# A half-product stage of a decoder layer: VectorE's low parts and token sums emitted in another place

## The chip, the core and the metric

The kernel runs on one core of one Trainium2 chip. The metric is the device time of one execution in microseconds (us). The engines are named as in the profile: PE is TensorE (PEld its weight loads), DVE is VectorE, ACT is ScalarE, POOL is GpSimd, SP is SyncE, which here only issues transfers.

## The reference

One layer of a hybrid decoder on 512 tokens of width 1024, in float32. A first sub-layer mixes tokens (RWKV-7 and sparse attention side by side); the change does not touch it. The second is a gated MLP with a short causal convolution:

```python
h = rms_norm(x, norm_ffn_pre[l])
u = causal_dwconv(h @ ffn_up[l], ffn_conv_w[l], ffn_conv_b[l])   # width 3, 2 * D_FF channels
u_gate, u_val = jnp.split(u, 2, axis=-1)
x = x + rms_norm((jax.nn.silu(u_gate) * u_val) @ ffn_down[l], norm_ffn_post[l])
```

D_FF is 2816, so the up projection makes 44 blocks of 128 channels, 22 for the gate and 22 for the value, and the kernel takes them as 22 pairs.

## The kernel before, in words

**Float32 out of two parts.** Every operand of a large product is kept as a high part and a low part: ACT copies the raw tile into a rounded type (the high part), and DVE or POOL subtracts that from the raw tile (the low part). A product is then three matmuls: high by high, high by low, low by high. So each weight tile costs one transfer, one ACT operation and one subtraction before PE can use it.

**The up projection.** Pairs 0 to 9 are computed directly. Pairs 10 to 21 (`SEVEN`) are computed by `seven` with seven half-size products in place of eight: tokens and weights are split in halves, sums and differences of weight halves (made earlier by transfers that add, `fsum`) are multiplied with sums and differences of token halves (`forms`), and the four quarters of the result are combined from the seven products. For pair j the weight forms are called `swj5, swj2, swj1, swj3, swj6, swj4, swj8`, in the order in which PE takes them. Each product is 12 matmuls of 128x128 by 128x256 (line 1567). The accumulators in PSUM are g (`sg` in the profile, the gate), v (`sv`, the value) and two helpers t[0], t[1] (`st`).

The seven products go: g left, t[0], v right, t[1], g left again, g right, t[1] again. Between them DVE combines (`add`, line 1572): u2 = t[0] - u2 (where ACT copied g left to u2 first), u4 = v + u2, v right = t[1] + u4, g right = g - u4, v left = t[1] + u2. In the profile u2 and u4 are `su`. The seventh product adds into t[1], so PE may start it only when DVE has read t[1] for v right; this is the one place in the loop where PE waits for DVE inside a pair.

**Weight forms.** `form_w` (line 1537 on) loads a form, and `split_to` makes its two parts: the high part on ACT (line 134), the low part on POOL for five of the seven (5, 2, 3, 6, 4) and on DVE for two (1 and 8), all on line 172. Eight buffers hold the forms, five in one pool and three in another, and a buffer comes free when PE has finished the product that used it. Five forms are begun before the first product; then each product begins one more (`next(coming)` in `prod`).

**After a pair.** The convolution: for g, then for v, ACT writes u (line 1619) and DVE adds two shifted products (lines 1620, 1621, `u<-sg,cvec,u` and `u<-sv,cvec,u`). Then ACT takes silu of the gate (line 1633), DVE multiplies gate and value into y (line 1635, `sv<-u,sg`), ACT makes its high part ah (line 1638), and DVE its low part al (line 1639). From pair 11 on three DVE operations make the token sums t24 for the down projection (lines 1647 to 1649, `t` in the profile), which SP stores to DRAM one pair later (line 1645).

**The order of the work.** The kernel is written as a program, and a scheduler puts each engine's instructions in a fixed order from dependences, the place where they are written, and estimated times; operations passed to `keep` stay in the order in which they are written. Each engine then runs its list strictly in order and waits by semaphores. Beside the loop POOL issues the transfers that sum the down weights (`ws`, line 272, `ds` in the profile); SP issues all weight loads. After pair 21 the down projection (`dn`, lines 1745 to 1747) begins at once.

Of the kernel before, what the change touches and what calls it, by code (L numbers as in the profile page):

```python
# [10 lines left out]
F32 = mybir.dt.float32  # L11
F32R = mybir.dt.float32r
AF = mybir.ActivationFunctionType
OP = mybir.AluOpType
# [4 lines left out]
S = 512  # L19
# [33 lines left out]
def hybrid_layer(ctx: ExitStack, tc: tile.TileContext, a, out, dbg=None, stop=None):  # L53
# [112 lines left out]
    def split_to(src, hi, lo, name, n, eng=None, p=None, late=False, tag="raw", bufs=RAWB):  # L166
        raw = (p or wp).tile([128, n], F32, tag=tag, name=name + "r", bufs=bufs)
        sy.dma_start(raw, src)
        i = act(hi, raw, AF.Copy)
        if late:  # L170
            tc.keep_in_program_order(i)
        (eng or po).tensor_tensor(lo, raw, hi.bitcast(F32), op=OP.subtract)
# [1306 lines left out]
    with pool("ff") as ff:  # L1479
# [58 lines left out]
        def form_w(src, name, eng):  # L1538
            n = next(ring)
            p_, tags, b = (wp, ("raw", "whi", "wlo"), (RAWB, WB)) if n % 8 % 3 == 1 else (sw, ("sraw", "shi", "slo"), (4, 5))  # L1540
            hi = p_.tile([128, 512], F32R, tag=tags[1], name=name + "h", bufs=b[1])
            lo = p_.tile([128, 512], F32R, tag=tags[2], name=name + "l", bufs=b[1])
            split_to(src, hi, lo, name, 512, eng, p_, late=n < 5, tag=tags[0], bufs=b[0])
            return hi, lo

        def form_seq():
            for j in SEVEN:
# [10 lines left out]
        def seven(j):  # L1558
            def tok(r, c):
                return quarter(h2h, r, c), quarter(h2l, r, c)  # L1560

            def prod(p, x, first=True, last=True):
                w = ahead.pop(0)
                for k in range(hf):
                    ks = slice(k * 128, k * 128 + 128)
                    for n, (y, z) in enumerate(((0, 0), (0, 1), (1, 0))):
                        te.matmul(p, w[y][:, ks], x[z][:, k, :], start=first and k + n == 0,  # L1567
                                  stop=last and k == hf - 1 and n == 2, skip_group_check=True)
                next(coming, None)

            def add(o_, x, y, op=OP.add):
                ve.tensor_tensor(o_, x, y, op=op)

            g, v, t = (pj if j % 2 else px)(f"sg{j}"), (pj if j % 2 else py)(f"sv{j}"), [pz(f"st{j}{i}") for i in range(2)]
            u2, u4 = (sw.tile([128, 256], F32, tag=f"u{i}", name=f"su{i}{j}", bufs=1) for i in (2, 4))
            prod(g[:, lft], tok(0, 0))
            prod(t[0][:, lft], forms[1])
            sc.activation(u2, g[:, lft], AF.Copy)
            add(u2, t[0][:, lft], u2, OP.subtract)
            prod(v[:, rgt], forms[0])  # L1580
            add(u4, v[:, rgt], u2)
            prod(t[1][:, rgt], forms[2])
            prod(g[:, lft], tok(1, 0), first=False)
            add(v[:, rgt], t[1][:, rgt], u4)
            prod(g[:, rgt], tok(1, 1))
            add(g[:, rgt], g[:, rgt], u4, OP.subtract)
            prod(t[1][:, rgt], forms[3], first=False)
            add(v[:, lft], t[1][:, rgt], u2)
            return g, v

        side = token_forms()
        sctx2 = ExitStack()
        for j in range(22):
            us = []
            sv_ = None
            if j == 2:
                sw = pool("sw", "right", sctx2)
            if j == SEVEN[0]:
                for _ in side:
                    pass  # L1600
            if j in SEVEN:
                sv_ = seven(j)
            for x in range(2):
                blk = 2 * j + x
                if blk < NU:
                    p = pu4[blk]
                    half_up(blk, 1)
                elif sv_ is not None:
                    p = sv_[x]
                else:  # L1610
                    wh, wl = after.get(blk) or split_w(upw(blk), f"up{blk}")
                    p = ((pj, px, py, pz)[blk % 4] if j < SEVEN[0] else pj)(f"pu{blk}")
                    mm3(p, wslice(wh), wslice(wl), lambda k: h2h[:, k, :], lambda k: h2l[:, k, :])
                if blk == 2 * SEVEN[0] - 1:
                    for _ in range(5):
                        next(coming)
                cv = blk * 4
                u = fu.tile([128, S], F32, tag=f"u{x}", name=f"u{blk}", bufs=2)
                sc.activation(u, p, AF.Identity, scale=cvec[:, cv + 2:cv + 3], bias=cvec[:, cv + 3:cv + 4])  # L1619
                ve.scalar_tensor_tensor(u[:, 1:], p[:, :S - 1], cvec[:, cv + 1:cv + 2], u[:, 1:], op0=OP.mult, op1=OP.add)  # L1620
                ve.scalar_tensor_tensor(u[:, 2:], p[:, :S - 2], cvec[:, cv:cv + 1], u[:, 2:], op0=OP.mult, op1=OP.add)
                us.append(u)
                if j < SEVEN[0]:
                    for _ in range(1):
                        next(side, None)
                if (j > 2 or x == 0 if j < SEVEN[0] else x == 0 and j < 19):
                    next(ws, None)
            if sv_ is None:
                sc.activation(us[0], us[0], AF.Silu)
                (ve if j > SEVEN[0] - 3 else po).tensor_tensor(us[1], us[0], us[1], op=OP.mult)  # L1630
                y = us[1]
            else:
                sc.activation(sv_[0], us[0], AF.Silu)
                y = sv_[1] if j >= KH else us[1]
                ve.tensor_tensor(y, us[1], sv_[0], op=OP.mult)
            if j < KH:
                ve.tensor_tensor(y[:, rgt], y[:, rgt], y[:, lft], op=OP.subtract)
            sc.activation(ah[:, j, :], y, AF.Copy)
            ve.tensor_tensor(al[:, j, :], y, ah[:, j, :].bitcast(F32), op=OP.subtract)
            if j >= KH:  # L1640
                if j == KH:
                    t2ctx = ExitStack()
                    t2 = pool("t2", "left", t2ctx)
                else:
                    sy.dma_start(t24d[j - 1 - KH], t24)
                t24 = t2.tile([128, S], F32, tag="t24", name=f"t24{j}", bufs=2)
                ve.tensor_tensor(t24[:, lft], y[:, rgt], ah[:, j - KH, rgt].bitcast(F32), op=OP.subtract)
                ve.tensor_tensor(t24[:, lft], t24[:, lft], al[:, j - KH, rgt].bitcast(F32), op=OP.subtract)
                ve.tensor_tensor(t24[:, rgt], y[:, lft], t24[:, lft], op=OP.subtract)
            if j == 1:  # L1650
                f4ctx.close()
        po.dma_start(t24d[21 - KH], t24)
        ring = itertools.count()

# [264 lines left out]
```

## Time and profile before

| | us |
|---|---|
| median of 3 runs | 1137.9 (1136.57 to 1139.19) |
| the profiled execution | 1133.54, its span 1131.5 |
| pairs 10 to 21, from 899.08 to 1019.15 of the span | 120.1 |
| PE busy over the span | 1110.3 (98%) |
| DVE, ACT, POOL busy over the span | 750.4, 639.2, 613.5 |

The profile is one execution with the time and length of each instruction, and a chain of work that ended last, followed back from the end. An engine's instruction begins in the record a little before its neighbour ends, since they overlap by some 0.08 us on DVE; so a length of time on an engine is best read from start to start. Durations on POOL are rough. The program's tiles carry numbers in the kernel that the profile mostly leaves out: `sv<-st,su` is the read of t[1] for v right and, later in the same pair, the one for v left.

### The profile page before, as it was taken

What the parts mean: (1) busy time and instruction counts of PE and PEld (TensorE: products, weight loads), DVE (VectorE), ACT (ScalarE), POOL (GpSimd) and SP (SyncE); (2) the same over time, 40 slices, a digit from 0 to 9 for tenths busy, and PEclk for the clock granted to TensorE, in tenths of its full rate; (3) what the DMA queues carried; (4) which work ended last, traced back from release to release, by engine and by line L of the source; (5) the groups of instructions that cost most, each with busy time, mean ns of one, the idle gap of its engine ahead of it and who ended that gap; (6) DMA issues with size and microseconds to landing.
All of it is one profiled execution on the core that took longest, in us unless ns stands there. A gap on an engine that the chain in (4) does not pass through costs nothing.

```text
span 1131.5 us, 21237 instructions
## 1 busy us (share of the span) xinstructions
PE 1110.3 (98%) x7704; PEld 909.6 (80%) x7704; DVE 750.4 (66%) x1432; ACT 639.2 (56%) x1258; POOL 613.5 (54%) x615
## 2 busy tenths in 40 slices
PE   9999999999999999999999999999999999999997
PEld 7888888877888887766666777888888899998885
DVE  4236664735666552597787754755785699997986
ACT  6447763554666434386675654543554576665554
POOL 4346674535666453566545543540578777753431
PEclk9999999999999999999999999999999999999999
DMA  7524468632666896516576465777568678968783
GB/s 256 144 81 124 141 166 217 182 104 86 182 146 172 235 242 216 132 48 194 171 218 181 127 149 166 231 240 220 136 185 202 207 263 227 266 181 302 228 283 113
DMA packets 117002, 208.33 MB, mean 184 GB/s; under 512 B 37025, under 2 KB 39905, under 8 KB 110754
## 3 DMA queue, kind: packets, MB, share of 16 engines
q1 hardware_dynamic: 93538, 144.05, 40.6%
q0 software_dynamic: 7504, 48.50, 18.4%
q10 hardware_dynamic: 15856, 14.42, 4.0%
q8 instruction: 61, 1.00, 0.4%
q14 instruction: 43, 0.35, 0.1%
HBM read 179.60 MB, written 72.35 MB: 223 GB/s over the span
## 4 chain that ended last, share of the span: by engine, by line
PE 87%; DVE 5%; DMA 3%; POOL 2%; issue 1%; ACT 1%; SPq 0%; DVEq 0%; POOLq 0%; ACTq 0%
PE st L1567 4%; PE sg L1567 3%; PE dn L1745 3%; PE dn L1746 3%; PE dn L1747 3%; PE gt L348 3%; PE o L1218 3%; PE gt L349 3%; PE gt L350 3%; PE pt L150 3%; PE ub L1276 3%; PE pu L234 2%; PE ub L1278 2%; PE pu L232 2%; PE pu L233 2%; PE ub L1277 2%
## 5 line engine op out<-in xcount | busy, mean ns | idle before, releaser
L1166 ACT ACTIVATE p<-p,stt 128x384 f32<-128x384 f32 (+3 forms) x128 | 70.6, 554 | 33.4 <-DVE stt L1164 30.8
L1164 DVE CUSTOM_DVE_ANT_0 p<-s,rh 128x384 f32<-128x384 f32 (+3 forms) x128 | 59.2, 484 | 21.5 <-PE s L1150 17.9
L1138 POOL TENSOR_SCALAR p<-p,stt 128x512 f32<-128x512 f32 (+1 forms) x64 | 39.3, 622 | 38.7 <-DVE stt L1131 24.5
L1746 PE MATMUL dn<-hl,ah 128*128 128x512 f32 x148 | 57.6, 389 | 0.0
L1747 PE MATMUL dn<-hh,al 128*128 128x512 f32 x148 | 57.6, 389 | 0.0
L1745 PE MATMUL dn<-hh,ah 128*128 128x512 f32 x148 | 57.2, 389 | 0.0
L150 PE MATMUL pt<-ident,p 128*128 128x128 f32 x320 | 44.3, 273 | 1.2 <-DVE p L1140 1.2
L1157 PE MATMUL s<-kst,qs 128*128 128x512 f32 (+1 forms) x128 | 38.8, 394 | 5.8 <-DVE stt L1164 5.6
L150 PEld LDWEIGHTS pt<-ident,p 128*128 128x128 f32 x320 | 37.8, 141 | 6.9 <-DVE p L1140 1.6
L1218 PE MATMUL o<-PT,vt 128*64 128x384 f32 (+3 forms) x256 | 41.0, 443 | 0.0
L1209 ACT ACTIVATE PT<-pt 128x512 f32<-128x512 f32 x48 | 27.5, 587 | 10.4 <-PE pt L150 10.3
L1157 PEld LDWEIGHTS s<-kst,qs 128*128 128x128 f32 x128 | 21.2, 189 | 15.0 <-DVE stt L1164 11.8
L1140 DVE TENSOR_SCALAR p<-p,stt 128x512 f32<-128x512 f32 (+1 forms) x64 | 32.3, 532 | 0.7
L1747 PEld LDWEIGHTS dn<-hh,al 128*128 128x128 f32 x148 | 27.8, 188 | 5.8
L1745 PEld LDWEIGHTS dn<-hh,ah 128*128 128x128 f32 x148 | 27.8, 188 | 5.8
L1746 PEld LDWEIGHTS dn<-hl,ah 128*128 128x128 f32 x148 | 27.8, 188 | 5.7
L1218 PEld LDWEIGHTS o<-PT,vt 128*64 128x64 f32 x256 | 16.3, 136 | 18.3 <-issue 16.0
L272 POOL DMA_DIRECT2D ds<-in_down_dram x36 | 25.6, 710 | 7.3 <-DMA ds<-ds 7.3
L1620 DVE SCALAR_TENSOR_TENSOR u<-pu,cvec,u 128x511 f32<-128x511 f32 x20 | 15.0, 748 | 19.2 <-ACT u L1619 19.2
L1211 DVE COPY PT<-pt 128x512 f32<-128x512 f32 x32 | 21.8, 680 | 8.6 <-PE pt L150 8.5
L251 POOL DMA_DIRECT2D fs<-in_up_dram x36 | 26.0, 731 | 0.5 <-issue 0.4
L868 ACT ACTIVATE UV<-xs 64x256 f32<-64x256 f32 x16 | 6.0, 378 | 35.7 <-PE xs L861 35.3
(2206 smaller groups left out, 4242.4 us busy)
## 6 DMA issues: line engine op xcount, KB each, us to landing
fs<-in_up_dram POOLq DMA_DIRECT2D x36, 512.0 KB, 6.5
ds<-in_down_dram POOLq DMA_DIRECT2D x30, 512.0 KB, 6.1
fs<-fs POOLq DMA_DIRECT2D x12, 512.0 KB, 4.4
ds<-ds POOLq DMA_DIRECT2D x10, 512.0 KB, 5.7
gtd<-gt ACTq DMA_DIRECT2D x16, 256.0 KB, 4.8
qs<-qd SPq DMA_DIRECT2D x32, 128.0 KB, 3.6
g<-gtd SPq DMA_DIRECT2D x16, 256.0 KB, 3.6
t24d<-t SPq DMA_DIRECT2D x10, 256.0 KB, 5.4
```

The costliest lines, as they stand in the source:

```text
L150: return te.transpose(o, i, ident)
L348: te.matmul(p, wh(k), hh[:, k, :], start=k == 0, stop=False)
L349: te.matmul(p, wh(k), hl[:, k, :], start=False, stop=False)
L1138: po.tensor_scalar(o.pe[e, b, k], o.pe[e, b, k], w, 1.0, op0=OP.mult, op1=OP.mult)
L1157: m = te.matmul(s_[:, :n], qt, kt[:, x, b, :n], start=x == 0, stop=x == 1)
L1164: ve.tensor_tensor_reduce(sb, parts[b], rh[e][:, (3 - qb) * 128:], -1.0, BIG, OP.add, OP.min, st[e][:, 0, i:i + 1])
L1166: sc.activation(sb, sb, AF.Exp, scale=-1.0, bias=st[e][:, 0, i:i + 1], accum_out=st[e][:, 1, i:i + 1])
L1218: te.matmul(acc[e * 64:e * 64 + 64, j * 128:], vt[:, j, b * 256 + g * 64:b * 256 + g * 64 + 64], m[e][:, c:c + n], start=False, stop=k == ...
L1567: te.matmul(p, w[y][:, ks], x[z][:, k, :], start=first and k + n == 0, stop=last and k == hf - 1 and n == 2, skip_group_check=True)
L1745: te.matmul(p, xh, w[0], start=first, stop=False)
L1746: te.matmul(p, xh, w[1], start=False, stop=False)
L1747: te.matmul(p, xl, w[0], start=False, stop=last)
```

## The change

It moves three groups of DVE's instructions in the program, all in the stage of the half-product pairs.

- The low parts that DVE makes (forms 1 and 8, from the second pair of forms on) are no longer emitted with their high parts. They are put in a list `lows`, and `flush` emits them at two places in `seven`: behind the addition to v right and behind the one to v left. They are kept in the written order.
- The low part al and the three token sums of a pair are no longer emitted at the end of that pair. They are put in a list `deferred`, and `settle` emits them in the next pair, behind the addition to v right. (For pairs before 10 and for pair 21 they are emitted at once.)
- During the first pair each product begins two forms, until seven are begun ahead instead of five.

No operation, transfer or buffer is added or removed.

```diff
-            split_to(src, hi, lo, name, 512, eng, p_, late=n < 5, tag=tags[0], bufs=b[0])
+            if n < 5 or eng is po:
+                split_to(src, hi, lo, name, 512, eng, p_, late=n < 5, tag=tags[0], bufs=b[0])
+            else:
+                raw = p_.tile([128, 512], F32, tag=tags[0], name=name + "r", bufs=b[0])
+                sy.dma_start(raw, src)
+                sc.activation(hi, raw, AF.Copy)
+                lows.append((lo, raw, hi))
             return hi, lo
+
+        lows = []
+
+        def flush():
+            while lows:
+                lo, raw, hi = lows.pop(0)
+                keep(ve.tensor_tensor(lo, raw, hi.bitcast(F32), op=OP.subtract))
...
                 next(coming, None)
+                if j == SEVEN[0] and len(ahead) < 7:
+                    next(coming, None)
...
             add(v[:, rgt], t[1][:, rgt], u4)
+            settle()
+            flush()
             prod(g[:, rgt], tok(1, 1))
             add(g[:, rgt], g[:, rgt], u4, OP.subtract)
             prod(t[1][:, rgt], forms[3], first=False)
             add(v[:, lft], t[1][:, rgt], u2)
+            flush()
             return g, v
+
+        hold, deferred = [], []
+
+        def settle():
+            while deferred:
+                j, y = deferred.pop(0)
+                ve.tensor_tensor(al[:, j, :], y, ah[:, j, :].bitcast(F32), op=OP.subtract)
+                if j >= KH:
+                    if j == KH:
+                        t2ctx = ExitStack()
+                        hold[:] = [pool("t2", "left", t2ctx), t2ctx, None]
+                    else:
+                        sy.dma_start(t24d[j - 1 - KH], hold[2])
+                    t24 = hold[2] = hold[0].tile([128, S], F32, tag="t24", name=f"t24{j}", bufs=2)
+                    ve.tensor_tensor(t24[:, lft], y[:, rgt], ah[:, j - KH, rgt].bitcast(F32), op=OP.subtract)
+                    ve.tensor_tensor(t24[:, lft], t24[:, lft], al[:, j - KH, rgt].bitcast(F32), op=OP.subtract)
+                    ve.tensor_tensor(t24[:, rgt], y[:, lft], t24[:, lft], op=OP.subtract)
...
             sc.activation(ah[:, j, :], y, AF.Copy)
-            ve.tensor_tensor(al[:, j, :], y, ah[:, j, :].bitcast(F32), op=OP.subtract)
-            if j >= KH:
...
+            deferred.append((j, y))
+            if sv_ is None or j == 21:
+                settle()
...
+        t2, t2ctx, t24 = hold
```

What the scheduler makes of it is seen in the order of the built programs. The first place is DVE in the pair 17, before the change: from y of pair 16 (`sv<-u,sg`) over u4 and the reads of t[1] to the convolution of pair 17.

```order
L1635 TENSOR_TENSOR sv_10904<-u_11046,sg_10903 128x512
L1572 TENSOR_TENSOR su_11064<-sv_11060,su_11063 128x256
L172 TENSOR_TENSOR sw181l<-sw181r,sw181h 128x512
L1639 TENSOR_TENSOR al<-sv_10904,ah 128x512
L1647 TENSOR_TENSOR t_11055<-sv_10904,ah 128x256
L1572 TENSOR_TENSOR sv_11060<-st_11062,su_11064 128x256
L1648 TENSOR_TENSOR t_11055<-t_11055,al 128x256
L1649 TENSOR_TENSOR t_11055<-sv_10904,t_11055 128x256
L1572 TENSOR_TENSOR sg_11059<-sg_11059,su_11064 128x256
L172 TENSOR_TENSOR sw188l<-sw188r,sw188h 128x512
L1572 TENSOR_TENSOR sv_11060<-st_11062,su_11063 128x256
L1620 SCALAR_TENSOR_TENSOR u_11197<-sg_11059,cvec,u_11197 128x511
```

The same stretch of DVE after the change (line numbers are those of the changed kernel):

```order
L1670 TENSOR_TENSOR sv_10910<-u_11058,sg_10909 128x512
L1587 TENSOR_TENSOR su_11070<-sv_11066,su_11069 128x256
L1614 TENSOR_TENSOR al<-sv_10910,ah 128x512
L1587 TENSOR_TENSOR sv_11066<-st_11068,su_11070 128x256
L1622 TENSOR_TENSOR t_11166<-sv_10910,ah 128x256
L1623 TENSOR_TENSOR t_11166<-t_11166,al 128x256
L1624 TENSOR_TENSOR t_11166<-sv_10910,t_11166 128x256
L1557 TENSOR_TENSOR sw181l<-sw181r,sw181h 128x512
L1587 TENSOR_TENSOR sg_11065<-sg_11065,su_11070 128x256
L1655 SCALAR_TENSOR_TENSOR u_11209<-sg_11065,cvec,u_11209 128x511
L1587 TENSOR_TENSOR sv_11066<-st_11068,su_11069 128x256
L1557 TENSOR_TENSOR sw188l<-sw188r,sw188h 128x512
```

sw181l went from ahead of al to behind the three t operations, the first read of t[1] went ahead of all three, and sw188l went from between sg and u to behind u and the second read.

The second place is DVE at the first half-product pair, number 10, before:

```order
L172 TENSOR_TENSOR sw108l<-sw108r,sw108h 128x512
L1620 SCALAR_TENSOR_TENSOR u_9959<-pu_9904,cvec,u_9959 128x511
L1621 SCALAR_TENSOR_TENSOR u_9959<-pu_9904,cvec,u_9959 128x510
L1630 TENSOR_TENSOR u_9959<-u_9887,u_9959 128x512
L1572 TENSOR_TENSOR su_9973<-st_9971,su_9973 128x256
L1637 TENSOR_TENSOR u_9959<-u_9959 128x256
L172 TENSOR_TENSOR sw111l<-sw111r,sw111h 128x512
L1572 TENSOR_TENSOR su_9974<-sv_9970,su_9973 128x256
L1639 TENSOR_TENSOR al<-u_9959,ah 128x512
L1572 TENSOR_TENSOR sv_9970<-st_9972,su_9974 128x256
L1572 TENSOR_TENSOR sg_9969<-sg_9969,su_9974 128x256
```

and after, from u4 of that pair on:

```order
L1587 TENSOR_TENSOR su_9974<-sv_9970,su_9973 128x256
L1614 TENSOR_TENSOR al<-u_9959,ah 128x512
L1587 TENSOR_TENSOR sv_9970<-st_9972,su_9974 128x256
L1557 TENSOR_TENSOR sw108l<-sw108r,sw108h 128x512
L1557 TENSOR_TENSOR sw111l<-sw111r,sw111h 128x512
L1587 TENSOR_TENSOR sg_9969<-sg_9969,su_9974 128x256
```

Both low parts now stand between the read of t[1] and sg; sw108l is the low part of the form that the pair's seventh product uses.

The third place is POOL, with the low parts of pair 18 and a transfer of the down sums (`ds`), before:

```order
L172 TENSOR_TENSOR sw183l<-sw183r,sw183h 128x512
L172 TENSOR_TENSOR sw186l<-sw186r,sw186h 128x512
L272 DMA ds_157<-in_down_dram 64x2048
L172 TENSOR_TENSOR sw184l<-sw184r,sw184h 128x512
L172 TENSOR_TENSOR sw195l<-sw195r,sw195h 128x512
```

and after:

```order
L172 TENSOR_TENSOR sw183l<-sw183r,sw183h 128x512
L172 TENSOR_TENSOR sw186l<-sw186r,sw186h 128x512
L172 TENSOR_TENSOR sw184l<-sw184r,sw184h 128x512
L272 DMA ds_157<-in_down_dram 64x2048
L172 TENSOR_TENSOR sw195l<-sw195r,sw195h 128x512
```

The transfer now stands behind sw184l instead of in front of it. On ACT the high part of form 2 of the next pair (sw182h) moved ahead of the copy `su<-sg` and of silu; SP's loads change places by one or two. PE's order does not change.

More of the change, by code (lines that the diff above doesn't have):

```diff
@@ L1638, in hybrid_layer @@
             sc.activation(ah[:, j, :], y, AF.Copy)
-            ve.tensor_tensor(al[:, j, :], y, ah[:, j, :].bitcast(F32), op=OP.subtract)
-            if j >= KH:
[L1641 to L1649, printed above, removed]
+            deferred.append((j, y))
+            if sv_ is None or j == 21:
+                settle()
             if j == 1:
                 f4ctx.close()
+        t2, t2ctx, t24 = hold
         po.dma_start(t24d[21 - KH], t24)
```

## The prediction

> **What bounds the kernel now.** I read the page first, then the chain that ended last, then busy time in two stretches, then DVE, ACT and POOL in order of time. The profiled execution took 1133.54 us, 2.0 us more than its span:
>
> ```profile
> span 1131.5 us, 21237 instructions
> ```
>
> The chain is PE almost everywhere. These pieces (start, length, what) are the twelve half-product pairs, seven products of 12 matmuls each, and their end, where the down projection (dn) begins:
>
> ```profile
> 899.08 1.41 PE sg L1567 x12
> ...
> 907.44 1.36 PE st L1567 x12
> ...
> 938.00 1.44 PE sg L1567 x12
> ...
> 1006.22 0.68 DVE al L1639
> ...
> 1007.23 0.35 DVE sv L1572
> 1007.62 1.70 PE st L1567 x12
> ...
> 1019.15 0.23 PE dn L1745
> ```
>
> From 899.08 to 938.00 four pairs pass without a stop: 38.92 / 4 = 9.73 us each, the time of PE's own work. Twelve would take 116.8 us; they took 120.1 (to 1019.15). So **3.3 us** is all that the change can win here. Near 1007 the chain leaves PE for DVE: al, then sv (the read of t[1] that lets PE's seventh product overwrite it). The weight loads of that product waited so four times:
>
> ```profile
> PEld st L1567 <- DVE sv L1572: 2.5, 4, 0.9
> ```
>
> Why is DVE late? Columns: PE, PEld, DVE, ACT and POOL busy with counts, clock, DMA share, GB/s:
>
> ```profile
> 899.00:957.00 58.00, 57.97 (x498) 57.74 (x497) 54.10 (x89) 38.93 (x68) 42.10 (x35) 1.00 0.84 255
> 957.00:1019.00 62.00, 60.35 (x514) 59.69 (x513) 57.78 (x98) 41.29 (x74) 41.85 (x33) 1.00 0.75 217
> ```
>
> DVE is 93% busy in both. PE has the larger share, but DVE has so little air that its order of work decides whether PE stops. One cycle of DVE (start, length, line, what):
>
> ```profile
> 971.50 0.75 DVE L1620 SCALAR_TENSOR_TENSOR u<-sv,cvec,u 128x511 f32<-128x511 f32 x1 [0.20 <-ACT u L1619]
> ...
> 972.95 0.42 DVE L1572 TENSOR_TENSOR su<-st,su 128x256 f32<-128x256 f32 x1
> 973.28 0.69 DVE L1635 TENSOR_TENSOR sv<-u,sg 128x512 f32<-128x512 f32 x1
> 973.87 0.42 DVE L1572 TENSOR_TENSOR su<-sv,su 128x256 f32<-128x256 f32 x1
> 974.21 1.75 DVE L172 TENSOR_TENSOR sw181l<-sw181r,sw181h 128x512 fp32r<-128x512 f32 x1
> 975.88 0.68 DVE L1639 TENSOR_TENSOR al<-sv,ah 128x512 fp32r<-128x512 f32 x1
> 976.48 0.41 DVE L1647 TENSOR_TENSOR t<-sv,ah 128x256 f32<-128x256 f32 x1
> 976.81 0.41 DVE L1572 TENSOR_TENSOR sv<-st,su 128x256 f32<-128x256 f32 x1
> 977.14 0.41 DVE L1648 TENSOR_TENSOR t<-t,al 128x256 f32<-128x256 f32 x1
> 977.59 0.42 DVE L1649 TENSOR_TENSOR t<-sv,t 128x256 f32<-128x256 f32 x1
> 977.93 0.42 DVE L1572 TENSOR_TENSOR sg<-sg,su 128x256 f32<-128x256 f32 x1
> 978.26 1.45 DVE L172 TENSOR_TENSOR sw188l<-sw188r,sw188h 128x512 fp32r<-128x512 f32 x1
> 979.63 0.42 DVE L1572 TENSOR_TENSOR sv<-st,su 128x256 f32<-128x256 f32 x1
> 979.97 0.73 DVE L1620 SCALAR_TENSOR_TENSOR u<-sg,cvec,u 128x511 f32<-128x511 f32 x1
> 980.74 0.75 DVE L1621 SCALAR_TENSOR_TENSOR u<-sg,cvec,u 128x510 f32<-128x510 f32 x1
> 981.40 0.74 DVE L1620 SCALAR_TENSOR_TENSOR u<-sv,cvec,u 128x511 f32<-128x511 f32 x1
> ```
>
> From 971.50 to 981.40 it runs back to back in 9.90 us, over PE's 9.73. Two of the rows are long: the weight low parts sw181l (1.75) and sw188l (1.45). al, as wide, takes 0.68. POOL explains it:
>
> ```profile
> 974.11 1.29 POOL L172 TENSOR_TENSOR sw183l<-sw183r,sw183h 128x512 fp32r<-128x512 f32 x1
> 975.37 1.73 POOL L172 TENSOR_TENSOR sw186l<-sw186r,sw186h 128x512 fp32r<-128x512 f32 x1
> ...
> 979.76 1.30 POOL L172 TENSOR_TENSOR sw195l<-sw195r,sw195h 128x512 fp32r<-128x512 f32 x1 [0.61 <-ACT sw195h L134]
> ```
>
> sw181l begins while POOL's sw183l runs (to 975.40) and ends at 975.96, 0.56 behind it; POOL's next, sw186l, ends 1.14 behind sw181l. The two take turns, and only where a DVE operation reads SBUF twice: t<-t,al does too, and in an earlier pair it took 1.51 against POOL's sw136l, ending 0.28 behind it:
>
> ```profile
> 925.07 1.51 DVE L1648 TENSOR_TENSOR t<-t,al 128x256 f32<-128x256 f32 x1
> ...
> 925.01 1.29 POOL L172 TENSOR_TENSOR sw136l<-sw136r,sw136h 128x512 fp32r<-128x512 f32 x1
> ```
>
> **The change, part by part.** No operation is added or removed; the order on DVE is. (1) sw?1l goes from ahead of al to behind the three t operations. (2) sv<-st (the read PE waits for) goes ahead of those. (3) sw?8l goes from in front of the u that follows sg to behind it. (4) On POOL the down-sum DMA goes behind sw?4l. (5) sw108l moves behind the first sv read. (6) The two more weight forms ahead, and su behind sw?2h on ACT.
>
> What (1) and (3) uncover are waits for ACT that the low parts hid. al needs ah, u needs ACT's u of sg:
>
> ```profile
> 974.00 0.60 ACT L1638 ACTIVATE ah<-sv 128x512 fp32r<-128x512 f32 x1 [0.19 <-DVE sv L1635]
> 974.49 0.62 ACT L134 ACTIVATE sw186h<-sw186r 128x512 fp32r<-128x512 f32 x1
> ...
> 978.38 0.78 ACT L1619 ACTIVATE u<-sg,cvec 128x512 f32<-128x512 f32 x1 [0.69 <-DVE sg L1572]
> 979.06 0.62 ACT L134 ACTIVATE sw195h<-sw195r 128x512 fp32r<-128x512 f32 x1
> ```
>
> Where no low part stands between, DVE already idles there, once each:
>
> ```profile
> 1010.62 0.75 DVE L1620 SCALAR_TENSOR_TENSOR u<-sg,cvec,u 128x511 f32<-128x511 f32 x1 [0.26 <-ACT u L1619]
> ...
> 1027.30 0.69 DVE L1639 TENSOR_TENSOR al<-sv,ah 128x512 fp32r<-128x512 f32 x1 [0.67 <-ACT ah L1638]
> ```
>
> So I rebuild DVE's cycle in the new order, start to start, low parts at 0.60 (0.68 less the 0.08 that neighbours overlap). u to su 0.66; su 0.33; second u 0.78 (it follows directly what it feeds, as 979.97 to 980.74); sv<-u,sg to al 1.35 (0.69, then ah 0.60, with 0.06 of passing on; su fills a part); al 0.60; sv 0.33; t, t, t 0.44, 0.45, 0.34; sw?1l 0.60; sg to u 1.27 (0.42, ACT 0.78, passing on); u 0.66; sv 0.34; sw?8l 0.60; u 0.66. Sum **9.41 us** without a port wait. The old cycle with both low parts at 0.68 is 9.90 - 1.07 - 0.77 = 8.06. The new order costs 1.35 us of DVE per pair and leaves 0.32 of air instead of 1.67.
>
> Then the port. Count from the start of sv<-u,sg. ah starts at 0.72, sw?6h 0.49 later and takes 0.62, POOL's sw?6l starts 0.07 behind it (979.06 + 0.62 to 979.76): 1.91 to 3.21. t<-t,al arrives at 2.72, ends at 3.49 instead of 3.13: **0.36**. Now sw?4l is next, as the DMA no longer stands ahead of it: it ends 1.14 later, at 4.63. sw?1l arrives at 3.87, ends at 5.19 instead of 4.55: **0.64**. sg at 5.11, ACT's u 5.56 to 6.34, the next pair's sw?5h from 6.24, sw?5l 6.93 to 8.23; sw?8l arrives at 7.38, ends at 8.79 instead of 8.06: **0.73**. Together 1.73: 11.14 us per pair, PE's 9.73 exceeded by **1.41**.
>
> The lower price is the mean of all 24 low parts of DVE in this stage (columns: DVE busy, POOL busy, of line 172 alone):
>
> ```profile
> 895.00:1011.00 116.00, 28.49 (x24) 80.13 (x59) 1.00 0.81 243
> ```
>
> 28.49 / 24 = 1.19, so 0.51 of wait each, and a quarter of a microsecond for t<-t,al as an estimate: 10.68 us, 0.95 over. The Trainium skill (SBUF — State Buffer, Who interferes with whom) states that a DVE instruction with two SBUF inputs and a GpSimd one that reads SBUF exclude each other, and that issue order decides who blocks; by that rule the placed 1.41 holds, by the bare mean 0.95. The trace agrees with the exclusion (0.56 behind sw183l). I take 1.2, between them, since ACT's halves don't always come on the beat.
>
> Sum: pairs 13 to 20 have the full cycle, 8 x 1.2 = 9.6. At pair 10, (5): sw108l now follows the first sv (906.74) while POOL runs
>
> ```profile
> 906.13 1.44 POOL L172 TENSOR_TENSOR sw113l<-sw113r,sw113h 128x512 fp32r<-128x512 f32 x1 [2.49 <-PE sg L1567]
> ```
>
> to 907.57, so it ends at 908.1; PE's seventh product (907.44 above) stops 0.6, and sw111l behind it makes sg late, another 0.6 at pair 11 as an estimate. Pairs 11 and 12 carry no t operations (1.23 less): nothing. Pair 21 with the down weights' low parts: 1.0, an estimate from the loops before it. Together 11.8, less the 3.3 that is lost today: **+8.5 us**. On the profiled execution that is 1142.0; the median of the runs shown is 1137.9, 4.4 above it, and the forecast is made there: **1146.4**.
>
> At no cost: (2) alone is a gain of 0.33 that the late cycle swallows; (4) the DMA's landing is needed only in the down products; without that cover it would cost its 0.5 to 0.8 once; the store of t on SP waits for a t operation that comes no later than before. (6) PE's release of the eight buffers, not the depth, sets when a weight's high part is made, so I take zero; bounds: the one late load could vanish (less than 1 us of today's 3.3, not to be won twice), or SP's reordered loads could cost as much. su on ACT 0.63 later is hidden, since DVE needs it only after two u.
>
> **The rivals.** *The port stays free.* If POOL falls out of step, so that port waits stay below the 0.32 of air, PE never waits but at pair 10: 3.3 - 0.6 = 2.7 won, 1135.2. For it: early low parts of the old order ran unblocked. Against: POOL's line 172 is busy 80.13 of 116, and each DVE read comes just behind the ACT result that also starts POOL. *Half the waits.* At 0.7 per pair DVE takes 10.1, 0.4 over: 3.2 + 1.2 + 0.0 less 3.3 is +1.1: 1139.0. For it: the mean above is over both kinds of stretch. *The change does not do what it says* in part: the depth of seven may make no weight ready earlier; my sum counts on nothing from it, so that would still be 1146.4.
>
> **How the numbers follow.** The full cycle 0.72; free port 0.15; half waits 0.13. The forecast's own range: at least 0.6 over in eight pairs, 1.2 and 0.5 beside it, less 3.3, is +3.2; at most 1.41 in nine pairs, 1.8 at pairs 10 and 11 (the estimate doubled), 2.0 at pair 21, less 3.3, is +13.2: 1141 to 1151. With the free port left out and one more microsecond for the spread of the runs the range of 8 in 10 is 1136 to 1152. A measurement here tells about 0.2%, 2.3 us, from no change: faster 0.15, same 0.13, slower 0.72.
>
> **What would show it.** Right: DVE idle before u of sg (0.85) and al (0.35) in nearly each pair; sw?1l and sw?8l above 1.2 in pairs 13 to 20; PE's seventh product waiting for DVE's sv in each, pairs 10.7 to 11.2 us apart; sw108l near 908. Wrong: pairs 9.73 apart with low parts at 0.68, or PE waiting for weights instead.

## The result, and the profile after

The changed kernel takes 1153.5 us (median of 5, 1151.1 to 1155.4) against 1136.6 (median of 5, 1131.9 to 1139.2): the ratio is 1.0149, with a 95% interval of 1.0123 to 1.0175. It is slower by 16.9 us; the forecast was 8.5 slower, 1146.4, with a range that ended at 1152. The profiled execution took 1155.4, the longest of its five. Its span:

```profile
span 1153.6 us, 21223 instructions
```

Before, the stage of the half-product pairs took 120.2 us, from PE's first product of pair 10 (898.9) to the end of its last of pair 21 (1019.1); now it takes 138.0 (901.2 to 1039.2). The two profiled executions differ by 21.9 (1155.4 - 1133.5): the stage gives 17.8 of it, and all that lies around it 4.1 (2.3 ahead of it, where nothing was changed). So these two profiles stand further apart than the medians do.

In the chain of work that ended last, PE was nearly everything before. Now the chain runs along DVE, and one and the same operation (the read of t[1] for v left: start, length, what) comes back in it once a pair:

```profile
1009.15 0.42 DVE sv L1587
...
1020.34 0.42 DVE sv L1587
...
1031.54 0.42 DVE sv L1587
```

11.19 and 11.20 us: where nothing else disturbs it, a pair takes **11.20**, 1.47 over PE's 9.73. The waits between 901 and 1040 us (engine, line, waited for: total, times, longest); the first row stood at 2.5 us before:

```profile
PEld st L1580 <- DVE sv L1587: 18.2, 10, 3.4
...
DVE u L1655 <- ACT u L1654: 12.3, 12, 3.0
DVE al L1614 <- ACT ah L1673: 8.9, 11, 2.1
```

The second and third rows are the two waits that the moved low parts used to fill. One cycle of DVE (start, length, line, what, idle ahead of it):

```profile
970.98 0.42 DVE L1587 TENSOR_TENSOR sg<-sg,su 128x256 f32<-128x256 f32 x1
972.24 0.75 DVE L1655 SCALAR_TENSOR_TENSOR u<-sg,cvec,u 128x511 f32<-128x511 f32 x1 [0.85 <-ACT u L1654]
...
973.24 1.41 DVE L1557 TENSOR_TENSOR sw168l<-sw168r,sw168h 128x512 fp32r<-128x512 f32 x1
...
978.42 0.69 DVE L1614 TENSOR_TENSOR al<-sv,ah 128x512 fp32r<-128x512 f32 x1 [0.34 <-ACT ah L1673]
...
979.80 0.74 DVE L1623 TENSOR_TENSOR t<-t,al 128x256 f32<-128x256 f32 x1
...
980.92 1.33 DVE L1557 TENSOR_TENSOR sw171l<-sw171r,sw171h 128x512 fp32r<-128x512 f32 x1
982.18 0.42 DVE L1587 TENSOR_TENSOR sg<-sg,su 128x256 f32<-128x256 f32 x1
```

The idle times are 0.85 and 0.34, and t<-t,al, sw?1l and sw?8l are 0.33, 0.65 and 0.73 over their free lengths: the forecast's rows, to 0.03. sg to sg is 11.20.

Some pairs take longer still: pairs 14, 15 and 18 have 12.75, 12.89 and 13.27. In pair 15 ACT waits for a load, and ah, which stands behind that load's high part, is late (rows of ACT, then of DVE):

```profile
965.84 0.63 ACT L134 ACTIVATE sw163h<-sw163r 128x512 fp32r<-128x512 f32 x1 [2.14 <-DMA sw163r<-fs]
966.38 0.58 ACT L1673 ACTIVATE ah<-sv 128x512 fp32r<-128x512 f32 x1
```

```profile
966.99 0.69 DVE L1614 TENSOR_TENSOR al<-sv,ah 128x512 fp32r<-128x512 f32 x1 [1.77 <-ACT ah L1673]
967.60 0.42 DVE L1587 TENSOR_TENSOR sv<-st,su 128x256 f32<-128x256 f32 x1
```

PE's seventh product waits for that last row. So two costs show: a loop of 11.20, and late loads on top of it. The theory after this profile: the low parts' new place makes both. Its rivals are that al and the token sums come later, that more forms are begun ahead, or that the loads are late by themselves.

### The profile page after: what moved, and what is told of

Read it like the earlier page. It is cut to its first block, busy times and chain, and to the rows that moved or that the text cites. A ratio compares the mean times of both kernels' runs of the same rounds, so it can differ in the third digit from the quotient of the medians.

```text
span 1153.6 us, 21223 instructions
## 1 busy us (share of the span) xinstructions
PE 1116.1 (97%) x7704; PEld 912.0 (79%) x7704; DVE 758.3 (66%) x1432; ACT 637.8 (55%) x1258; POOL 611.9 (53%) x615
## 4 chain that ended last, share of the span: by engine, by line
PE 74%; DVE 11%; DMA 5%; issue 3%; POOL 3%; ACT 3%; SPq 0%; DVEq 0%; POOLq 0%; ACTq 0%
PE o L1218 3%; PE gt L348 3%; PE pt L150 3%; PE gt L350 3%; PE gt L349 3%; PE ub L1276 3%; PE pu L234 2%; PE ub L1278 2%; PE pu L232 2%; PE pu L233 2%; PE ub L1277 2%; PE v L348 2%; PE v L349 2%; PE v L350 2%; PE dn L1774 1%
## 5 line engine op out<-in xcount | busy, mean ns | idle before, releaser
L1157 PEld LDWEIGHTS s<-kst,qs 128*128 128x128 f32 x128 | 21.2, 189 | 15.1 <-DVE stt L1164 11.8
```

Source lines behind the costliest of these rows:

```text
L1157: m = te.matmul(s_[:, :n], qt, kt[:, x, b, :n], start=x == 0, stop=x == 1)
```

## The experiments

Each ran beside the kernel before on one chip; the ratios, with their 95% intervals, are to that kernel, whose medians there were 1135.2 to 1136.6 us.

### Which part of the change costs

**settle_only**: the low parts are made at once, as before; al and the token sums stay late, the depth stays.

```diff
-            if n < 5 or eng is po:
+            if True:
```

> Only al and the token sums are emitted late; both low parts stand where the kernel before has them, and seven forms are begun ahead. Theory A: DVE's cycle is that of before (9.9 us with port waits), with the read of t[1] up to 0.9 us earlier in it: 1133 to 1138 us, like before (1136.6) or up to 0.3% faster. Theory B: 1150 or more if the deeper queue of loads is what hurts. Theory C: like before.

1137.1 us, 1.0004 [0.9984, 1.0024]: no difference, so B, the deeper queue of loads by itself, falls.

**lows_only**: the low parts stay late, al and the token sums are emitted at once.

```diff
-            if sv_ is None or j == 21:
-                settle()
+            settle()
```

> Only the low parts are emitted late (with seven forms ahead); al and the token sums are emitted at the end of their pair as before. Theory A: the waits for ACT before al and u are open as in the changed kernel and the cycle stays near 11.2 us: 1150 to 1156 us. Theory B: 1150 to 1155 as well. Theory C: the port waits are about those of the changed kernel, 1150 to 1155.

1154.9 us, 1.0171 [1.0143, 1.0199]: the whole loss. All three of its theories allowed this, so what it tells is where the loss sits. In its trace regular pairs stand 11.52 apart.

**depth7_alone**: the kernel before with the two more forms ahead.

```diff
                 next(coming, None)
+                if j == SEVEN[0] and len(ahead) < 7:
+                    next(coming, None)
```

> The kernel before with nothing but the two more weight forms begun ahead. A (the depth costs nothing and gains nothing, since the release of the buffers sets when a weight's high part is made): as before, 1134 to 1138 us. B (loads issued in another order land later and stop the engines): 1139 to 1145.

1136.8 us, 0.9996 [0.9979, 1.0014]: A. The depth and the late al are free of cost where the low parts are made early; the low parts' place is the cause. No run has late low parts without the extra depth, so whether the two together make loads late is not known.

### Which of the two low parts

**sw8_back**: form 8's low part between sg and u again.

```diff
-            add(v[:, lft], t[1][:, rgt], u2)
             flush()
+            add(v[:, lft], t[1][:, rgt], u2)
```

> The changed kernel (1153.5 us) with one thing undone: the low part of form 8 stands between sg and u again. Theory A (DVE's cycle is the sum of its work, the two waits for ACT and the port waits): the wait of 0.85 us before u is filled by the low part, which there meets no POOL operation; the cycle falls from about 11.2 by 0.60 and 0.73 to 9.9 us, almost PE's 9.73, so the time falls to 1137 to 1143 us. Theory B (late weight loads hold ACT and with it everything; DVE's order matters little): 1150 to 1155. Theory C (only the port waits count, not the waits for ACT): only 0.73 of 1.73 us per pair goes, 1146 to 1149.

1146.5 us, 1.0101 [1.008, 1.0122]: 7 won, above what A named and inside C's range. DVE:

```profile
970.85 0.42 DVE L1587 TENSOR_TENSOR sg<-sg,su 128x256 f32<-128x256 f32 x1
971.19 0.68 DVE L1557 TENSOR_TENSOR sw168l<-sw168r,sw168h 128x512 fp32r<-128x512 f32 x1
972.12 0.75 DVE L1655 SCALAR_TENSOR_TENSOR u<-sg,cvec,u 128x511 f32<-128x511 f32 x1 [0.26 <-ACT u L1654]
```

The low part takes 0.68, with no turn to wait for, and the idle time falls from 0.85 to 0.26; C, which leaves that wait out, has no place for it. (In pairs 17 and 20 the two low parts change roles: sw?8l takes 1.37 and 1.45, sw?1l 0.68.) Undisturbed pairs take 9.8 to 10.4, where A had 9.9. In several of them PE now stops at another wait, its fifth product for ACT's copy `su` (0.2 to 0.3 us). And pairs 14, 15 and 18 take 13.23, 12.38 and 11.78, behind a late load; sw8_ah below tests whether that is the miss.

**sw1_back**: form 1's low part behind u4 and ahead of al again.

```diff
             add(u4, v[:, rgt], u2)
+            flush()
...
             settle()
-            flush()
```

> The changed kernel with another thing undone: the low part of form 1 stands between u4 and the read of t[1] again, ahead of al. Theory A: the wait of 0.34 us before al is filled, the low part meets the end of a POOL operation there (0.3 us) instead of 0.65; the cycle is about 10.2 us, 0.45 over PE's: 1143 to 1147 us. Theory B: 1150 to 1155. Theory C: 0.5 us of port wait per pair less, 1148 to 1150.

1147.0 us, 1.0111 [1.0092, 1.0129]: in A's range, but the trace shows another way there. The loop is as long as in the changed kernel:

```profile
963.59 1.50 DVE L1623 TENSOR_TENSOR t<-t,al 128x256 f32<-128x256 f32 x1
...
972.50 1.00 DVE L1557 TENSOR_TENSOR sw171l<-sw171r,sw171h 128x512 fp32r<-128x512 f32 x1
...
974.80 1.50 DVE L1623 TENSOR_TENSOR t<-t,al 128x256 f32<-128x256 f32 x1
```

974.80 - 963.59 is 11.21. al idles no longer, sw?1l is down from 1.33 to 1.00, but t<-t,al now meets POOL's work and takes 1.50 in place of 0.74. What the idle time gave back, the turns took. Most of the 6.5 us won is in pairs 14, 15 and 18, which take 11.20 each here: no load of a form 3 is late. The loop can cost in full without the loads.

### Turns with POOL

**no_pool**: POOL makes no low parts; DVE's order is that of the changed kernel. It leaves out the low parts of five forms in seven, with the high part in their place in the third matmul.

```diff
+            if eng is po:
+                raw = p_.tile([128, 512], F32, tag=tags[0], name=name + "r", bufs=b[0])
+                sy.dma_start(raw, src)
+                i = sc.activation(hi, raw, AF.Copy)
...
+                return hi, hi
...
-            if n < 5 or eng is po:
+            if n < 5:
```

> The changed kernel without any low part on POOL: the third matmul of five forms in seven takes the high part again, and the low parts of those five forms are left out. VectorE's order is that of the changed kernel. A (the moved low parts uncover waits for ACT, and turns with POOL at SBUF then carry the cycle over PE's time): without POOL both of VectorE's low parts take 0.68, t<-t,al 0.42, its cycle is some 9.41 us, under PE's 9.73, though VectorE still idles 0.85 ahead of u and 0.34 ahead of al; pairs 9.7 to 9.8 apart, 1134 to 1138 us, perhaps 1 to 3 more where a late load still stands in front of ah on ACT. B (the waits for ACT alone hold the pair): still over 10.5 us per pair, 1145 to 1150. C (late loads are most of it): pairs 14, 15 and 18 as long as in the changed kernel, 1140 to 1145 at least.

1143.9 us, 1.0057 [1.0041, 1.0073], above A's range and inside C's. The loop is what A says, though:

```profile
971.06 0.75 DVE L1662 SCALAR_TENSOR_TENSOR u<-sg,cvec,u 128x511 f32<-128x511 f32 x1 [0.85 <-ACT u L1661]
...
972.05 0.68 DVE L1564 TENSOR_TENSOR sw168l<-sw168r,sw168h 128x512 fp32r<-128x512 f32 x1
...
976.50 0.69 DVE L1621 TENSOR_TENSOR al<-sv,ah 128x512 fp32r<-128x512 f32 x1 [0.34 <-ACT ah L1680]
...
977.89 0.43 DVE L1630 TENSOR_TENSOR t<-t,al 128x256 f32<-128x256 f32 x1
...
978.69 0.68 DVE L1564 TENSOR_TENSOR sw171l<-sw171r,sw171h 128x512 fp32r<-128x512 f32 x1
...
980.61 0.75 DVE L1662 SCALAR_TENSOR_TENSOR u<-sg,cvec,u 128x511 f32<-128x511 f32 x1 [0.90 <-ACT u L1661]
```

The same idle times stand there, but each operation takes its free length, and the cycle (971.06 to 980.61) is 9.55, under PE's 9.73. In the chain, from the seventh product of pair 14 to that of pair 17:

```profile
959.80 1.36 PE st L1587 x12
...
988.92 1.44 PE st L1587 x12
```

29.12 / 3 = 9.71: PE does not stop, and C's long pairs 14, 15 and 18 are not there. The time above A's range is one stop of this kernel alone, some 9 us in pair 10, where a load landed very late. POOL, without low parts to make, had issued six transfers of the down sums in a row just before (ACT, then POOL):

```profile
912.90 0.63 ACT L1545 ACTIVATE sw112h<-sw112r 128x512 fp32r<-128x512 f32 x1 [10.14 <-DMA sw112r<-fs]
```

```profile
895.27 3.66 POOL L272 DMA_DIRECT2D ds<-in_down_dram  x6
```

So bare waits alone do not cost; with the turns they do.

**one_in**: DVE's two low parts become a product of the raw weight with a constant, so they read SBUF once; the subtraction is left out in those two forms.

```diff
-                keep(ve.tensor_tensor(lo, raw, hi.bitcast(F32), op=OP.subtract))
+                keep(ve.tensor_scalar(lo, raw, 2.0 ** -12, None, op0=OP.mult))
```

> The changed kernel, POOL at work as ever, but VectorE's two low parts are not the difference of the raw weight and its high part: they are a product of the raw weight with a constant, so they read SBUF once instead of twice; what that leaves out is the subtraction in two of seven forms. Order, counts and POOL's work stay. A (VectorE and POOL take turns only where VectorE reads SBUF twice): both take their own time, at most 0.7 us with no wait, t<-t,al alone still waits some 0.3 to 1, and the cycle is 9.8 to 10.3 at most; 1134 to 1142 us, a late load included. B (any VectorE operation on SBUF alone waits for POOL): 1.2 to 1.4 each as now, 1150 to 1155 us.

1149.2 us, 1.0121 [1.01, 1.0142]: between A and B. DVE, then POOL:

```profile
975.94 0.42 DVE L1557 TENSOR_SCALAR sw171l<-sw171r 128x512 fp32r<-128x512 f32 x1
...
978.54 1.29 DVE L1557 TENSOR_SCALAR sw178l<-sw178r 128x512 fp32r<-128x512 f32 x1
```

```profile
978.11 1.43 POOL L172 TENSOR_TENSOR sw185l<-sw185r,sw185h 128x512 fp32r<-128x512 f32 x1
```

A falls: this operation, with one input, takes 0.42 alone and 1.29 beside POOL, and ends 0.29 behind POOL's. So the prediction's "only where a DVE operation reads SBUF twice" is too narrow. It was also the wrong substitute for the question. The Trainium skill (SBUF — State Buffer, Who interferes with whom) states that a `tensor_scalar` can run in a mode that uses both of DVE's ports, and that it then takes turns with GpSimd too; the trace agrees, with 0.42 here for what took 0.68 with two inputs, and with the wait. The rows of the changed kernel have operations that read one tile from SBUF and the other from PSUM, and they do stay clear: t<-sv,ah took its 0.41 at 931.09, while POOL's sw136l ran.

### The late loads

**ah_first**: on ACT the high part of form 3 stands behind ah.

```diff
+            if n >= 5 and n % 7 == 3 and last_ah:
...
+                i = act(hi, raw, AF.Copy)
+                tc.add_manual_dep(i.ins, last_ah[-1].ins.name, ..., reason="behind ah")
```

> The changed kernel with one order on ACT undone: the high part of a pair's form 3 stands behind ah, not ahead of it, so a late load of that form can't hold up ah, al and the read that PE waits for. A (the regular loop costs 11.20 us per pair, the late loads another 4 to 5 us in pairs 14, 15 and 18): those pairs come down to 11.2 to 11.6 and the time to 1147 to 1150 us, 4 to 6 under the changed kernel. B (those pairs are long for the load itself: PE needs that weight, or the turn of the engines is lost in any case): no change, 1152 to 1155.

1148.5 us, 1.01 [1.0085, 1.0116]: A, 5.0 under the changed kernel. Pairs 14, 15 and 18 take 11.39, 11.40 and 11.42, and al waits 0.4 us at most, where the longest wait was 2.1:

```profile
DVE al L1622 <- ACT ah L1681: 3.8, 11, 0.4
```

But pair 17 now takes 12.98, where it had 11.54: a late load of form 4 (3.6 us of waiting on ACT) stops it instead.

**sw8_ah**: this edit and sw8_back together.

> Two edits that ran alone, together: form 8's low part back between sg and u, and the high part of form 3 behind ah on ACT. A (the two costs are separate and add up: 10.3 us per pair with form 8's low part back, and the late loads in pairs 14, 15 and 18 on top of it, some 6 us in that profile): those pairs come down to 10.3 to 10.6, 1139 to 1143 us. B (the long pairs with form 8's part back have another cause): no change from it alone, 1145 to 1148.

1142.8 us, 1.0064 [1.0048, 1.008]: A. Pairs 14 and 15 take 10.60 and 10.52, so most of sw8_back's miss was the late loads; one load still stops pair 17 (12.58), and in most others PE waits 0.3 to 0.4 us for ACT's copy `su`.

Why are loads late? Rows of DVE and of SP in the changed kernel:

```profile
943.86 1.33 DVE L1557 TENSOR_TENSOR sw141l<-sw141r,sw141h 128x512 fp32r<-128x512 f32 x1
```

```profile
945.22 0.32 SPq L168 DMA_DIRECT2D sw153r<-fs  x1
```

sw153r is issued 0.03 us behind the end of sw141l. That low part is the last reader of a raw buffer; made later, it holds the buffer longer, and the load that needs it starts later. To test whether the sharing of the buffers matters, **after_alt** is the changed kernel with the raw buffers dealt evenly: before, five loads in eight shared one ring of four buffers, and three in eight the other.

```diff
+            rp, rtag = (wp, "raw") if (n % 2 == 0 if n >= 8 else n % 8 % 3 == 1) else (sw, "sraw")
...
-                raw = p_.tile([128, 512], F32, tag=tags[0], name=name + "r", bufs=b[0])
+                raw = rp.tile([128, 512], F32, tag=rtag, name=name + "r", bufs=4)
```

> The changed kernel with nothing but the raw buffers dealt evenly. A (the late loads come from buffers held longer, and are 4 to 5 us of the loss; the other 12 are the loop's order and the turns with POOL): pairs 11.2 apart throughout, 1146 to 1150 us. B (transfers land late whenever they are issued): 1151 to 1155 us. C (the loop too is held by loads): under 1145 us.

1148.1 us, 1.0101 [1.0082, 1.0119]: A. Pairs 13 to 20 take 11.20 to 11.24 each, and the longest wait of PE's weight loads for DVE is half of what it was:

```profile
PEld st L1581 <- DVE sv L1588: 14.4, 10, 1.7
```

So the late loads are 5.4 of the 16.9 us (1153.5 - 1148.1; the two intervals allow some 2 to 9), and the loop is the other 11.5.

That the buffers' sharing makes loads late is shown; how it does so is only in part what the theory says. The landing of the same load in the kernel before, the changed kernel and after_alt (the last number is us from issue to landing):

```profile
sw153r<-fs SPq DMA_DIRECT2D x1, 256.0 KB, 3.1
```

```profile
sw153r<-fs SPq DMA_DIRECT2D x1, 256.0 KB, 7.7
```

```profile
sw153r<-fs SPq DMA_DIRECT2D x1, 256.0 KB, 2.8
```

In pairs 15, 16, 18 and 19 the load of form 3 is issued 6.1 to 7.3 us before ACT is free for it in the kernel before, 5.5 to 6.0 in the changed one, 7.4 in after_alt. So it is issued 0.6 to 1.3 later than before; but it also takes 7.0 to 8.4 to land, against 3.0 to 4.4 before and 2.7 to 3.9 in after_alt. With the old landing times it would still have come in time. Slow landings as such are not new: from pair 13 on, of the loads whose landing the profiles show, 12 of 53 take over 6 us in the kernel before and 12 of 50 in the changed one. What the change moves is the loads that they fall on.

### Is there a better place?

**both_gap**: both low parts between sg and u, where DVE idles 0.85 us; those of pair 10 as in the kernel before.

```diff
-            if n < 5 or eng is po:
+            if n < 7 or eng is po:
...
             settle()
-            flush()
...
+            flush()
             add(v[:, lft], t[1][:, rgt], u2)
-            flush()
```

> The changed kernel with al, the token sums and the extra depth as they are, but both of VectorE's low parts between sg and the u that follows it, the place where VectorE otherwise idles 0.85 us for ACT; the two low parts of the first pair stay where the kernel before had them. A (what costs is the waits left bare and the turns with POOL, and the place decides both): VectorE's cycle is some 9.1 us with one turn behind POOL's form 4, at most 9.8 with a second, so PE hardly stops in pairs 12 to 20, which stand 9.7 to 9.9 apart; 1133 to 1137 us, the kernel before or up to 3 under it. B (any deferral of the low parts costs, since they hold their buffers longer and loads come late): 1142 or more, with ACT waiting for the load of a form 3 or 4.

1146.1 us, 1.0098 [1.0071, 1.0125]: B, with the late loads that B names. Undisturbed pairs take 9.7 to 10.0, so the order itself costs next to nothing any more. But the loads are late, and between 901 and 1035 us these waits stand out:

```profile
DVE al L1613 <- ACT ah L1672: 13.5, 11, 4.2
...
ACT sw153h L134 <- DMA sw153r<-fs: 4.5, 1, 4.5
...
ACT sw163h L134 <- DMA sw163r<-fs: 4.0, 1, 4.0
```

**both_gap_ah**: the same with form 3's high part behind ah.

> Both low parts between sg and u as in the run before it, and the high part of form 3 behind ah on ACT. A (the low parts' place has already taken VectorE off PE's path, and late loads are rare there): the same as with the low parts alone, within 2 us. B (late loads in front of ah are what is left): 1 to 4 us under it, 1131 to 1134 us.

1150.4 us, 1.013 [1.0111, 1.0149]: neither theory; it is slower by 4. DVE shows the new wait:

```profile
966.43 0.68 DVE L1565 TENSOR_TENSOR sw161l<-sw161r,sw161h 128x512 fp32r<-128x512 f32 x1
970.79 1.16 DVE L1565 TENSOR_TENSOR sw168l<-sw168r,sw168h 128x512 fp32r<-128x512 f32 x1 [3.69 <-ACT sw168h L1556]
```

The late load now holds form 8's high part, and DVE stands in front of form 8's low part for 3.69 us with the read that PE needs queued behind it. PE's fourth product of pairs 15 to 17, that of form 3, now starts 1.5 to 2.1 us late as well. In these runs an order on ACT only chose who waits.

**both_gap_alt**: both_gap with the raw buffers dealt evenly.

> Both low parts between sg and u, and the raw buffers dealt evenly: from the ninth form on, every second load goes to the other ring of four, where before five in eight shared four buffers and three in eight the other four. A (a load is late because its buffer, held by a low part made late, came free late): loads are issued 2 to 5 us earlier against their use, ACT no longer waits for them over 1 us, pairs 9.7 to 9.9 apart throughout, 1133 to 1138 us, down 8 to 13 from the same kernel with the old rings. B (transfers land late whenever they are issued): pairs 14, 15 and 18 as long as they were, 1143 to 1148 us.

1135.1 us, 11.0 under both_gap; 0.9991 [0.9979, 1.0003] to the kernel before, which is no difference that can be told. A in the time, and PE's wait for DVE is all but gone (14.4 us in after_alt):

```profile
PEld st L1581 <- DVE sv L1588: 1.5, 3, 0.8
```

Two of A's signs fail: ACT still waits up to 3.1 us for a load of form 4, and pair 19 takes 10.53. But the high part of form 3 stands ahead of ah, and its load in pairs 15, 16, 18 and 19 is issued 1.3 to 3.6 us earlier than in both_gap, counted from when ACT is free for it, and lands in 2.9 to 4.7; in both_gap three of those four took 7.4 to 8.1.

**before_alt**: the kernel before with the even rings.

> The kernel before with nothing but the raw buffers dealt evenly. A (part of its own stops in pairs 15 to 17 and 20 follows from loads that come late): 1 to 3 us under the kernel before, 1133 to 1135.5 us. B (its stops are turns with POOL alone): no change, 1135.5 to 1138 us.

1135.4 us, 0.9995 [0.998, 1.001]: no difference that can be told. The number stands on the border of the two ranges, so it decides neither A nor B; an effect of 1 to 3 us is as large as the interval.

**pool_six**: settle_only with form 1's low part on POOL.

```diff
-                for x, eng in (((0, 0), po), (2, po), (1, ve), (3, po), ...
+                for x, eng in (((0, 0), po), (2, po), (1, po), (3, po), ...
```

> The changed kernel with its low parts where they were before (ahead of al and ahead of u), al and the token sums late, and one thing new: form 1's low part is made by POOL and not by VectorE, so POOL makes six of seven and VectorE one. A (what stops PE now and then is a VectorE low part that waits its turn behind POOL's): VectorE's cycle falls by about 1 us to under 9 us, no stops in pairs 13 to 20, PE's stage 117 to 118.5 us, 1133 to 1136 us, 1 to 3 under the kernel before. B (POOL's longer chain, 7.8 us of each 9.73, only takes more turns with t<-t,al and form 8, and al now waits bare for ah): the same as before or up to 4 us slower, 1136 to 1141.

1139.3 us, 1.002 [1.0001, 1.0038]: B's range; if anything it is slower. No version beats the kernel before by more than can be told.

## Why the prediction was wrong

The direction was right, and so was the mechanism of the loop; the size was half. Two steps failed above all: the price of 1.2 us per pair, and the zero put on step (6), where the late loads were. The sum had 11.8 us over PE's own 116.8 in the stage; the profile has 21.2 (138.0 - 116.8). The pairs' lengths below are those from one seventh product of PE to the next. By its steps:

- **The cycle of 9.41 without turns** holds: idle times 0.85 and 0.34 as forecast, and no_pool's cycle, with the same idle times and no turn, fits into PE's 9.73.
- **The turns with POOL, 1.73, and 11.14 us per pair** hold: 1.71 in the rows, 11.20 per pair. The first failed step is the next one, "I take 1.2, between them". The mean of the old order's low parts (1.19) was no lower bound for the new: DVE's 23 late low parts average 31.73 / 23 = 1.38, since each meets POOL at the same phase in every pair (from 13 to 20, sw?1l takes 1.31 to 1.34 and sw?8l 1.41 or 1.42). At the placed 1.41, pairs 13 to 20 would have come to 11.3 in place of 9.6; in after_alt, which shows the loop alone, they take 89.8, 11.9 over 8 x 9.73. That is 2.3 of the error of 9.4.

The group of those low parts (DVE busy, count, of line 1557 alone):

```profile
895.00:1045.00 150.00, 31.73 (x23) 0.99 0.69 201
```

- **"Pairs 11 and 12 carry no t operations (1.23 less): nothing"** failed. Pair 12 took 11.46, 1.7 over, though from read to read no token sum stands in its cycle:

```profile
919.30 0.42 DVE L1587 TENSOR_TENSOR sv<-st,su 128x256 f32<-128x256 f32 x1
920.08 1.01 DVE L1614 TENSOR_TENSOR al<-u,ah 128x512 fp32r<-128x512 f32 x1 [0.35 <-ACT ah L1673]
921.01 1.78 DVE L1557 TENSOR_TENSOR sw121l<-sw121r,sw121h 128x512 fp32r<-128x512 f32 x1
...
924.98 1.41 DVE L1557 TENSOR_TENSOR sw128l<-sw128r,sw128h 128x512 fp32r<-128x512 f32 x1
...
930.15 0.69 DVE L1614 TENSOR_TENSOR al<-sv,ah 128x512 fp32r<-128x512 f32 x1 [0.34 <-ACT ah L1673]
930.76 0.42 DVE L1587 TENSOR_TENSOR sv<-st,su 128x256 f32<-128x256 f32 x1
```

919.30 to 930.76 is 11.46: al stands in it twice, since the first comes behind the read, held up by the subtraction between the halves of y that later pairs don't have (line 1672, ahead of the rows shown); and this one reads y from SBUF, where later pairs have it in PSUM, so it waits for POOL (1.01 in place of 0.69). sw121l, at 1.78, waits longer than in later pairs. What the t operations left free, the turns took in part, as in sw1_back.

- **Pairs 10 and 11, 0.6 each**: too much. (Form 8's low part of pair 10 is moved too: the test in the code is n < 5, and it is the seventh form.) sw108l began at 908.48, near the 908 of the forecast, but by luck: the stage begins 2.3 us later in this profile, and counted from its start sw108l came 0.6 earlier than forecast. So pair 10's seventh product began on time, PE's weight loads waited only 0.26 for sw108l, and pair 11 took 10.18, 0.45 over. Pair 21, guessed at 1.0 over, took 10.62, 0.9 over; in after_alt it took 11.53, so this hit is partly luck as well.
- **"(6) ... so I take zero"** is the largest miss. The depth alone is zero (depth7_alone), but the step looked at the depth and not at what a late low part does to the loads: it holds its raw buffer, the loads are issued at other times, that of form 3 0.6 to 1.3 us later, and in the new pattern the slow landings fall on form 3, whose high part stands ahead of ah on ACT. That is 5.4 us by after_alt, 5.0 by ah_first; in the profiles, pairs 13 to 20 took 95.7 with it and 89.8 without. The step had SP's issues as a queue; it did not follow who frees the buffers that they wait for. Together the terms make 2.3 + 5.9 + 1.7, less 0.9 that was forecast too much at pairs 10, 11 and 21: 9.0 of the error of 9.4.
- **The rivals**: a free port (1135.2) and half waits (1139.0) are out; the turns came in every pair. That the depth does nothing was right.

What stays open: why a load lands 3 us after its issue in one place and 8 in another. The late ones come several at a time, with the down sums' transfers beside them. In no_pool the last of those is issued before 907 us, and from pair 13 on no weight load whose landing the profile shows takes over 5.2 us. That points at these transfers, but no_pool changes more than that, and in sw1_back, with the same transfers, none takes over 7. No run took the transfers alone away.

## What to carry to other kernels

An operation that a busy engine does while it waits for another engine's result is free only in that place: before moving it, write down the wait it covers, and what other engine's work it will meet in the new place. Where two engines take turns, price the new place by its own phase, not by the mean of the old one; and taking time off such a loop may only lengthen a turn. Follow each moved operation to the buffers that it is the last reader of: the next load into them is issued at another time and may land at another speed, and the queue in which its consumer stands decides who pays.

## What the runs showed that was not expected

A turn may be skipped. In settle_only a low part of DVE stood behind two of POOL's in a row and took 3.28 us, 0.57 past the end of the second (DVE, then POOL):

```profile
995.97 3.28 DVE L172 TENSOR_TENSOR sw201l<-sw201r,sw201h 128x512 fp32r<-128x512 f32 x1
```

```profile
995.99 1.46 POOL L172 TENSOR_TENSOR sw203l<-sw203r,sw203h 128x512 fp32r<-128x512 f32 x1
997.28 1.40 POOL L172 TENSOR_TENSOR sw206l<-sw206r,sw206h 128x512 fp32r<-128x512 f32 x1
```

It is no single event: in depth7_alone the same low part took 3.30, and in pool_six a t<-t,al took 3.11. Lengths on POOL are rough, and why a turn is skipped no run shows. And the loop locks: after_alt's eight pairs from 13 to 20 lie within 0.04 us of each other. The likely reason, argued and not tested, is that POOL's work starts from ACT results that DVE itself sets off.
